# A hybrid S5 / gMLP encoder on one core: second tokens turned inside a product, last columns in two parts, S5 tiles pipelined, and 512 columns per matmul for the weights' first part

## The chip, the core and the metric

One NeuronCore of one Trainium2 chip runs the whole kernel. It has TensorE (matmul; the profile shows its weight loads apart as PEld), VectorE (DVE), ScalarE (ACT), GpSimd (POOL) and SyncE (SP), each with an instruction queue of its own, and 16 DMA engines. The metric is the device time in microseconds, the median of several runs. Beside it stands one profiled execution, from which all rows are read.

## The reference

A trunk of two layers over 256 tokens of 1024 channels, in float32. Each layer is three sub-layers, each followed by a layer normalisation of `alpha*x + sublayer(x)`: a SwiGLU feed-forward layer, a mixer (S5 state space model in layer 0, gMLP spatial gating in layer 1), and a second feed-forward layer.

```python
def _swiglu(x, w_in, w_out):
    gate, up = jnp.split(x @ w_in, 2, axis=-1)
    return (jax.nn.silu(gate) * up) @ w_out

for i in range(DEPTH):                       # DEPTH = 2, D_MODEL = 1024, D_FF = 2816
    h = _layernorm(DN_ALPHA * h + 0.5 * _swiglu(h, ffn_w_in[i, 0], ffn_w_out[i, 0]), ...)
    mix = _s5_mixer(h, ...) if i % 2 == 0 else _gmlp_mixer(h, ...)
    h = _layernorm(DN_ALPHA * h + mix, ...)
    h = _layernorm(DN_ALPHA * h + 0.5 * _swiglu(h, ffn_w_in[i, 1], ffn_w_out[i, 1]), ...)

# the end of the S5 mixer
y = jax.nn.gelu(y)
z = y * jax.nn.sigmoid(y @ w_glu + b_glu)
return z @ w_out
```

So the six sub-layers are FFN, S5, FFN, FFN, gMLP, FFN; the four feed-forward layers are called the first to the fourth below.

## The kernel before

Every product is done in three float32r products: an operand x is split into `hi`, its rounding to float32r, and `lo = x - hi`, and x*w is `xh*wh + xh*wl + xl*wh`. So each weight block of 128 x 2048 numbers that a DMA brings (`raw`) is rounded on ACT (`hi`) and subtracted on DVE (`lo`). `Stream` (`ws`) does that in order: `tick` finishes the subtraction that is pending, starts loads, and splits the next block while at most five split blocks are held; `done` gives a block free.

The tokens stand as `h[0]` and `h[1]`, 128 tokens each on the partitions. For a product over channels they are turned: `make_xt(t)` transposes `h[t]` on TensorE into a PSUM tile `tps`, ACT copies it (`xth`, line 192) and DVE subtracts (`xtl`, line 193). `xt` holds both token halves t and both parts j as `[128, t, j, 8 blocks k, 128]`.

A feed-forward layer goes over 11 chunks c of 256 hidden columns. In the three later layers the chunks 0 and 1 are done by `step_in(c, t)` for each token half with tokens as the stationary operand (lines 201 to 203, 512 columns); the second half of the tokens is turned after `step_in(1, 0)`. From chunk 2 on, and in the first layer from chunk 1 on, `chunk_in` has the weights as the stationary operand: for each of 2 m and 2 g (gate and up) and 8 k there are three products of 256 columns (both token halves), lines 208 to 210, one after another in one PSUM half-bank each. `act_t` then does silu on ACT (line 397) and the product with the up half on DVE (line 398); `split_gt` splits the result into `gt` (lines 406 and 407). `step_out` accumulates `gt` against the out weights into `acc` two chunks later, and `close` does the last three chunks' out products, the residual sum, the normalisation and, in between, the turning of the first tokens for the next sub-layer.

The normalisation of a token half (`layernorm_half`, `layernorm`, `rstd_of`, `normalize`): residual sum (line 239) and statistics (240) for each 512 columns, aggregate (247), on POOL the offset by epsilon (221) and the power -0.5 (222), meanwhile on DVE the subtraction of the mean (228), then the scaling (231). After the last one, two DMAs store each token half.

At the end of the S5 layer, `finish(n)` makes eight tiles of 128 channels ready for the out product: product with the gate (1164), rounding (1168 on DVE for three tiles, 1170 on ACT for five), remainder (1171). Two `rest(1)` between them do halves of a waiting weight split (119).

The order on every engine is that in which the program is written (a manual schedule); SBUF and PSUM tiles come from rotating pools (`mm_p`: four PSUM banks).

## Time and profile before

| | |
|---|---|
| median of 3 runs | 971.5 us (970.46 to 971.52) |
| profiled execution | 971.83 us, its span 969.7 us |
| busy, share of the span | TensorE 97%, weight loads 88%, DVE 67%, ACT 44%, POOL 17% |
| three 256-column products, lines 208 to 210 | 1184 each, 283 ns each |
| three 512-column out products of the FFNs, lines 201 to 203 | 352 each, about 390 ns each |
| read from HBM | 184.07 MB, 200 GB/s over the span with what is written |

The span is the time from the first to the last instruction. Durations of matmuls overlap, since they are pipelined: the distance between two starts says what one costs. Idle time of an engine costs something only where it ends on the path that the result waits for.

### The profile page before, as it was taken

How to read it: one execution, taken by the hardware profiler on the slowest of the kernel's cores; microseconds unless marked ns; L12 is line 12 of the kernel's file. 1: busy time of each engine (PE TensorE's matmuls, PEld its weight loads, DVE VectorE, ACT ScalarE, POOL GpSimd, SP SyncE). 2: the span in 40 equal slices, each digit the busy share in tenths (PEclk: the TensorE clock that was granted, in tenths of full speed). 3: DMA queues.
4: the chain of work that ended last, by engine and by line, in shares of the span. 5: the costliest groups of instructions: out<-in, count | busy, mean ns of one | idle time of the engine just before them, and what ended most of it. 6: DMA issues, size and time to landing. Idle time of an engine off the chain costs nothing.

```text
span 969.7 us, 16611 instructions
## 1 busy us (share of the span) xinstructions
PE 944.7 (97%) x6988; PEld 857.9 (88%) x6988; DVE 650.9 (67%) x805; ACT 426.5 (44%) x504; POOL 162.8 (17%) x240
## 2 busy tenths in 40 slices
PE   7999999999999999999999999999999999999996
PEld 5999999978896799999987999999889879999995
DVE  5889998787998774554667636455788866453635
ACT  5465347535342553434433534353445444444430
POOL 1888910011750100000001000000011010000001
PEclk9999999999999999999999999999999999999999
DMA  8887796958646566365547765636357468465521
GB/s 276 219 249 228 237 318 203 315 200 300 208 141 220 174 198 236 132 224 167 185 163 239 255 222 166 225 133 227 121 173 261 130 203 268 138 220 172 184 78 43
DMA packets 133898, 195.10 MB, mean 201 GB/s; under 512 B 7632, under 2 KB 104576, under 8 KB 133824
## 3 DMA queue, kind: packets, MB, share of 16 engines
q1 hardware_dynamic: 129152, 182.61, 56.8%
q0 software_dynamic: 4384, 10.92, 3.9%
q8 instruction: 54, 0.88, 0.4%
q10 hardware_dynamic: 288, 0.52, 0.1%
q14 instruction: 20, 0.16, 0.0%
HBM read 184.07 MB, written 9.96 MB: 200 GB/s over the span
## 4 chain that ended last, share of the span: by engine, by line
PE 68%; DVE 8%; ACT 2%; issue 1%; POOL 1%; DMA 1%; POOLq 0%; DVEq 0%; ACTq 0%
PE ips L210 11%; PE ips L209 11%; PE ips L208 11%; PE acc L201 7%; PE acc L202 7%; PE acc L203 7%; DVE lo L97 3%; PE pps L1080 2%; PE ips L203 1%; ACT hi L96 1%; DVE lo L89 1%; DMA raw<-in_s_w_in 1%; PE ips L201 1%; PE ips L202 1%; PE zps L209 1%
## 5 line engine op out<-in xcount | busy, mean ns | idle before, releaser
L210 PE MATMUL ips<-xt,lo 128*128 128x256 f32 x1184 | 335.2, 283 | 2.2 <-DVE lo L89 2.2
L208 PE MATMUL ips<-xt,hi 128*128 128x256 f32 x1184 | 335.4, 283 | 0.0
L209 PE MATMUL ips<-xt,hi 128*128 128x256 f32 x1184 | 335.0, 283 | 0.0
L89 DVE TENSOR_TENSOR lo<-raw,hi 128x2048 fp32r<-128x2048 f32 x107 | 242.9, 2291 | 8.7 <-ACT hi L88 8.3
L210 PEld LDWEIGHTS ips<-xt,lo 128*128 128x128 f32 x1184 | 227.1, 192 | 2.6 <-DVE lo L89 2.6
L208 PEld LDWEIGHTS ips<-xt,hi 128*128 128x128 f32 x1184 | 227.1, 192 | 1.5
L209 PEld LDWEIGHTS ips<-xt,hi 128*128 128x128 f32 x1184 | 227.1, 192 | 1.4
L88 ACT CAST hi<-raw 128x2048 fp32r<-128x2048 f32 x107 | 203.9, 1909 | 46.4 <-PE acc L203 26.6
L398 DVE TENSOR_TENSOR sgg<-ips,sgg 128x256 f32<-128x256 f32 x74 | 31.1, 420 | 166.1 <-ACT sgg L397 166.0
L201 PE MATMUL acc<-hi,gt 128*128 128x512 f32 x352 | 137.9, 392 | 0.2 <-ACT gt L406 0.2
L202 PE MATMUL acc<-lo,gt 128*128 128x512 f32 x352 | 137.4, 390 | 0.0
L203 PE MATMUL acc<-hi,gt 128*128 128x512 f32 x352 | 137.0, 389 | 0.0
L397 ACT ACTIVATE sgg<-ips 128x256 f32<-128x256 f32 x74 | 28.4, 383 | 216.4 <-PE ips L210 213.5
L221 POOL TENSOR_SCALAR rstd<-mv 128x1 f32<-128x1 f32 x14 | 10.4, 741 | 634.6 <-DVE mv L247 610.8
L97 DVE TENSOR_TENSOR lo<-raw,hi 128x2048 fp32r<-128x2048 f32 (+2 forms) x52 | 89.6, 1754 | 22.7 <-ACT hi L96 22.6
L203 PEld LDWEIGHTS acc<-hi,gt 128*128 128x128 f32 x352 | 66.1, 188 | 14.3 <-DVE gt L407 0.2
L201 PEld LDWEIGHTS acc<-hi,gt 128*128 128x128 f32 x352 | 66.2, 188 | 13.2 <-ACT gt L406 0.6
L202 PEld LDWEIGHTS acc<-lo,gt 128*128 128x128 f32 x352 | 66.3, 188 | 12.2
L96 ACT CAST hi<-raw 128x2048 fp32r<-128x2048 f32 (+2 forms) x52 | 74.5, 1482 | 4.2 <-DMA raw<-in_ffn_w_in 2.5
L407 DVE TENSOR_TENSOR gt<-sgg,gt 128x256 fp32r<-128x256 f32 x74 | 32.4, 438 | 61.8 <-ACT gt L406 61.8
L406 ACT CAST gt<-sgg 128x256 fp32r<-128x256 f32 x74 | 30.1, 406 | 58.2 <-DVE sgg L398 58.2
L201 PE MATMUL ips<-hi,xt 128*128 128x512 f32 x112 | 46.0, 410 | 3.6 <-ACT xt L192 2.3
(229 smaller groups left out, 1222.1 us busy)
## 6 DMA issues: line engine op xcount, KB each, us to landing
raw<-in_ffn_w_in SPq DMA_DIRECT2D x172, 512.0 KB, 5.7
raw<-in_ffn_w_out SPq DMA_DIRECT2D x44, 1024.0 KB, 5.1
raw<-in_g_w_in SPq DMA_DIRECT2D x8, 1024.0 KB, 6.0
rows<-w SPq DMA_DIRECT2D x8, 512.0 KB, 6.3
raw<-in_s_w_in SPq DMA_DIRECT2D x4, 1024.0 KB, 8.4
raw<-in_s_w_glu SPq DMA_DIRECT2D x4, 1024.0 KB, 5.0
w<-rows SPq DMA_DIRECT2D x8, 512.0 KB, 5.8
tc<-tc SPq DMA_DIRECT2D x16, 256.0 KB, 5.5
```

Source lines behind the costliest of these rows:

```text
L88: nc.scalar.copy(hi, raw)
L89: self.unfinished.append(lambda: nc.vector.tensor_tensor(lo, raw, hi.bitcast(F32), op=ALU.subtract))
L96: nc.scalar.copy(hi[:, s], raw[:, s])
L97: eng[p % len(eng)].tensor_tensor(lo[:, s], raw[:, s], hi[:, s].bitcast(F32), op=ALU.subtract)
L201: nc.tensor.matmul(ps, xh, wh, start=start, stop=False)
L202: nc.tensor.matmul(ps, xh, wl, start=False, stop=False)
L203: nc.tensor.matmul(ps, xl, wh, start=False, stop=stop)
L208: nc.tensor.matmul(ps, wh, xh, start=start, stop=False)
L209: nc.tensor.matmul(ps, wh, xl, start=False, stop=False)
L210: nc.tensor.matmul(ps, wl, xh, start=False, stop=stop)
L398: nc.vector.tensor_tensor(g, ps[:, 1], sg, op=ALU.mult)
L407: nc.vector.tensor_tensor(x[:, 1], g, x[:, 0].bitcast(F32), op=ALU.subtract)
```

## The change

Five edits.

1. In the later feed-forward layers chunks 2 to 10 go through `chunk_in2`: the weights' first part `wh` is multiplied with both parts of both token halves in one product of 512 columns (parts j side by side in a whole PSUM bank), and `wl` with the first part in one of 256 columns that adds to the first half of the bank. The two halves are added afterwards: an ACT copy of the second half to SBUF, and a DVE sum with the first, for gate and up each. The silu and the product with the up half then work from SBUF.
2. `make_xt(1)` at the start of these layers and of the gMLP is written into `step_in(1, 0)` / `step_v(1, 0)`, after the fifth of its eight k, ahead of the weight split that a `tick` issues there; the ticks of step (0, 0) split nothing.
3. `finish(n)` returns the remainder's instruction, which is issued after the next tile's product and rounding; for tiles 3 and 5 it is on POOL. `z` has four places instead of two. The two halves of a weight split come after tiles 4 and 5 instead of 1 and 3.
4. `rstd_of` adds epsilon on DVE instead of POOL.
5. The last normalisation has `close_last`: the last 512 columns of the last token half are accumulated for the last three chunks in two parts of 256 columns, in banks of their own, and the sum of the residual with what `acc` already holds is done before. The last step and its store are in three parts.

```diff
+    def mm2t(ps, wh, wl, k):
+        both = ps.rearrange("p j (t c) -> p j t c", t=2)
+        nc.tensor.matmul(both, wh, xt[:, :, :, k].rearrange("p t j c -> p j t c"), start=k == 0, stop=False)
+        nc.tensor.matmul(ps[:, 0], wl, xt[:, :, 0, k], start=False, stop=k == KD - 1)
...
-        nc.gpsimd.tensor_scalar(rstd[:, 0:1], mv[:, 1:2], eps, 1.0, op0=ALU.add, op1=ALU.mult)
+        nc.vector.tensor_scalar(rstd[:, 0:1], mv[:, 1:2], eps, 1.0, op0=ALU.add, op1=ALU.mult)
...
+    def close_last(acc, blocks, mm, gb, hscale, eps):
+        for t in range(2):
+            r = ln_p.tile([P, D], F32, tag="r", name="r", bufs=2)
+            parts = [(0, 512), (512, 512)] if t == 0 else [(0, 512), (512, 256), (768, 256)]
...
+            if t == 1:
+                s = slice(512, D)
+                nc.vector.scalar_tensor_tensor(r[:, s], in0=h[t][:, s], scalar=hscale, in1=acc[t][1], op0=ALU.mult, op1=ALU.add)
...
-        def step_in(c, t):
+        def step_in(c, t, mid=None, split=1):
             ps = mm_p.tile([P, 512], F32, tag="mm", name="ips")
-            in_mm(ids["in"][c], t, ps, range(4))
+            cut = 5 if mid else 4
+            in_mm(ids["in"][c], t, ps, range(cut))
+            if mid:
+                mid()
             if t:
                 finish_g()
-            ws.tick()
-            in_mm(ids["in"][c], t, ps, range(4, KD))
+            ws.tick(split)
+            in_mm(ids["in"][c], t, ps, range(cut, KD))
...
+        def chunk_in2(c):
+            for m in range(2):
+                sgg = g_p.tile([P, 2, SEQ], F32, tag="sgg", name="sgg")
+                for g in range(2):
+                    ps = mm_p.tile([P, 2, SEQ], F32, tag="mm", name="ips")
+                    for k in range(KD):
+                        wh, wl = ws.get(ids["in"][c][k // 4])
+                        s = slice(512 * (k % 4) + FC * g + P * m, 512 * (k % 4) + FC * g + P * m + P)
+                        mm2t(ps, wh[:, s], wl[:, s], k)
...
+                    split_gt()
+                    nc.scalar.copy(sgg[:, g], ps[:, 1])
+                    nc.vector.tensor_tensor(sgg[:, g], sgg[:, g], ps[:, 0], op=ALU.add)
+                    if g == 0:
+                        nc.scalar.activation(sgg[:, 0], sgg[:, 0], AF.Silu)
+                    else:
+                        nc.vector.tensor_tensor(sgg[:, 1], sgg[:, 1], sgg[:, 0], op=ALU.mult)
+                        later.append((new_gt(c, m), sgg[:, 1]))
...
-            step_in(0, 0)
-            step_in(1, 0)
-            make_xt(1)
+            step_in(0, 0, split=0)
+            step_in(1, 0, lambda: make_xt(1))
...
-            chunk_in(c)
+            (chunk_in if first else chunk_in2)(c)
...
-            z = buf["o"][n % 2][:, 0].rearrange("p q k -> p (q k)")
+            z = buf["o"][n % 2][:, n // 2 % 2].rearrange("p q k -> p (q k)")
...
-            V.tensor_tensor(yx(n, 1), z, yx(n, 0).bitcast(F32), op=SUB)
+            return lambda: (G if n in (3, 5) else V).tensor_tensor(yx(n, 1), z, yx(n, 0).bitcast(F32), op=SUB)
...
+        second = lambda: None
         for n in range(CT):
-            finish(n)
-            if n in (1, 3):
+            x = finish(n)
+            second()
+            second = x
+            if n in (4, 5):
                 rest(1)
+        second()
```

How the order moves, at three places. TensorE, where chunk 2 of the second feed-forward layer begins, behind the last products of chunk 1 (`ips` is the PSUM tile, `hi` and `lo` the parts of a weight block). Before:

```order
L201 MATMUL ips_3867<-hi48_3722,xt_96 128x512
L202 MATMUL ips_3867<-lo48_3723,xt_96 128x512
L203 MATMUL ips_3867<-hi48_3722,xt_96 128x512
L208 MATMUL ips_3915<-xt_96,hi49_3750 128x256
L209 MATMUL ips_3915<-xt_96,hi49_3750 128x256
L210 MATMUL ips_3915<-xt_96,lo49_3751 128x256
```

And now:

```order
L201 MATMUL ips_3867<-hi48_3722,xt_96 128x512
L202 MATMUL ips_3867<-lo48_3723,xt_96 128x512
L203 MATMUL ips_3867<-hi48_3722,xt_96 128x512
L216 MATMUL ips_3916<-xt_96,hi49_3795 128x512
L217 MATMUL ips_3916<-xt_96,lo49_3796 128x256
```

Three products per k became two, of which the first has 512 columns.

DVE at the start of the second feed-forward layer, from the last step of the S5 layer's normalisation (`h1`) on. Before:

```order
L231 SCALAR_TENSOR_TENSOR h1_95<-r_3668,rstd_3715,bet_3554 128x512 x2
L97 TENSOR_TENSOR lo48_3723<-raw48_3589,hi48_3722 128x512 x4
L97 TENSOR_TENSOR lo49_3751<-raw49_3602,hi49_3750 128x2048
L358 TENSOR_TENSOR sgg_3769<-ips_3737,sgg_3769 128x256
L358 TENSOR_TENSOR sgg_3797<-ips_3772,sgg_3797 128x256
L193 TENSOR_TENSOR xt_96<-tps_3800,xt_96 128x512
L193 TENSOR_TENSOR xt_96<-tps_3807,xt_96 128x512
```

And now:

```order
L238 SCALAR_TENSOR_TENSOR h1_95<-r_3668,rstd_3715,bet_3554 128x512 x2
L97 TENSOR_TENSOR lo48_3723<-raw48_3589,hi48_3722 128x512 x4
L399 TENSOR_TENSOR sgg_3762<-ips_3737,sgg_3762 128x256
L193 TENSOR_TENSOR xt_96<-tps_3781,xt_96 128x512
L193 TENSOR_TENSOR xt_96<-tps_3788,xt_96 128x512
L97 TENSOR_TENSOR lo49_3796<-raw49_3602,hi49_3795 128x2048
L399 TENSOR_TENSOR sgg_3811<-ips_3765,sgg_3811 128x256
```

The two subtractions for the turned tokens (`xt`) moved ahead of the whole weight split `lo49` and of the second step's gate product (`sgg`).

DVE in the middle of the S5 tiles (`rot` is z, `y` the activated output). Before, from tile 3's product:

```order
L1164 SCALAR_TENSOR_TENSOR rot<-rot,y 128x4x64
L1171 TENSOR_TENSOR xt<-rot,xt 128x2x128
L119 TENSOR_TENSOR lo_3490<-raw_3321,hi_3489 128x1024
L1164 SCALAR_TENSOR_TENSOR rot<-rot,y 128x4x64
L1171 TENSOR_TENSOR xt<-rot,xt 128x2x128
```

And now, from tile 3's product:

```order
L1236 SCALAR_TENSOR_TENSOR rot<-rot,y 128x4x64
L1243 TENSOR_TENSOR xt<-rot,xt 128x2x128
L1236 SCALAR_TENSOR_TENSOR rot<-rot,y 128x4x64
L119 TENSOR_TENSOR lo_3490<-raw_3321,hi_3489 128x1024
L1236 SCALAR_TENSOR_TENSOR rot<-rot,y 128x4x64
L1243 TENSOR_TENSOR xt<-rot,xt 128x2x128
```

The remainder that follows tile 3's product is now tile 2's; tile 3's own is on POOL, and the next one in the row is tile 4's.

More of the change, by code (lines that the diff above doesn't have):

```diff
@@ L274, in new_acc @@
         return [acc_p.tile([P, 512], F32, tag="acc", name="acc") for _ in range(2)]
+    def close_last(acc, blocks, mm, gb, hscale, eps):
+        for t in range(2):
+            r = ln_p.tile([P, D], F32, tag="r", name="r", bufs=2)
+            parts = [(0, 512), (512, 512)] if t == 0 else [(0, 512), (512, 256), (768, 256)]
+            step = parts[-1][1]
+            st = st_p.tile([P, D // step, 6], F32, tag="bst", name="bst")
+            if t == 1:
+                s = slice(512, D)
+                nc.vector.scalar_tensor_tensor(r[:, s], in0=h[t][:, s], scalar=hscale, in1=acc[t][1], op0=ALU.mult, op1=ALU.add)
+            for i, (c, w) in enumerate(parts):
+                s, n = slice(c, c + w), c // 512
+                ps = acc[t][n] if w == 512 else mm_p.tile([P, 512], F32, tag="mm", name="ops")[:, 0:w]
+                for j in range(len(blocks)):
+                    for kt in range(2):
+                        mm(j, t, n, kt, ps, (c % 512, w), w < 512 and j == 0 and kt == 0)
+                    if t == 0 and i == 0 and j < 2:
+                        ws.tick()
+                    if (t, i) == (1, len(parts) - 1):
+                        ws.done(blocks[j])
+                x, scale = (h[t], hscale) if w == 512 else (r, 1.0)
+                nc.vector.scalar_tensor_tensor(r[:, s], in0=x[:, s], scalar=scale, in1=ps, op0=ALU.mult, op1=ALU.add)
+                for x in range(c, c + w, step):
+                    nc.vector.bn_stats(st[:, x // step], r[:, x:x + step])
+            mv = st_p.tile([P, 2], F32, tag="mv", name="mv")
+            nc.vector.bn_aggr(mv, st)
+            rstd, (g, b) = rstd_of(mv, eps), gb
+            for n in range(2):
+                s = slice(512 * n, 512 * n + 512)
+                nc.vector.scalar_tensor_tensor(r[:, s], in0=r[:, s], scalar=mv[:, 0:1], in1=g[:, s], op0=ALU.subtract, op1=ALU.mult)
+            for i, (c, w) in enumerate(parts):
+                s = slice(c, c + w)
+                nc.vector.scalar_tensor_tensor(h[t][:, s], in0=r[:, s], scalar=rstd, in1=b[:, s], op0=ALU.mult, op1=ALU.add)
+                (nc.sync, nc.scalar)[i % 2].dma_start(out=out[0, P * t:P * t + P, s], in_=h[t][:, s])
@@ L276, in close @@
     def close(li, si, acc, blocks, mm, gb, hscale, eps, last):
+        if last:
+            return close_last(acc, blocks, mm, gb, hscale, eps)
         order = [(n, j) for n in range(2) for j in range(len(blocks))]
@@ L282, in close @@
                     mm(j, t, n, kt, acc[t][n])
-                    if (t, n, j, kt) == (1, 1, len(blocks) - 2, 0) and not last:
+                    if (t, n, j, kt) == (1, 1, len(blocks) - 2, 0):
                         make_xt(0, next_kind[li, si] == "s5")
@@ L290, in close @@
                     sums = layernorm_half(t, acc[t][0], 0, hscale)
-            if t == 1 and not last:
+            if t == 1:
                 ws.tick(1)
             layernorm(t, acc[t], gb, hscale, eps, sums)
-            if t == 1 and not last and next_kind[li, si] != "s5":
+            if t == 1 and next_kind[li, si] != "s5":
                 ws.tick(1, 4)
-            if last:
-                for n in range(2):
-                    s = slice(512 * n, 512 * n + 512)
-                    (nc.sync, nc.scalar)[n].dma_start(out=out[0, P * t:P * t + P, s], in_=h[t][:, s])
     def plan_ffn(li, fi, fine):
@@ L370, in step_in @@
                 done(ids["in"][c])
-            ws.tick()
+            ws.tick(split)
         def chunk_in(c):
@@ L439, in start_in, with mm_out @@
             done(ids["in"][0])
-        def mm_out(c, t, n, kt, ps):
+        def mm_out(c, t, n, kt, ps, cols=(0, 512), start=False):
             gh, gl = (gts[c, kt][:, j, P * t:P * t + P] for j in range(2))
             wh, wl = ws.get(ids["out"][c])
-            s = slice(D * kt + 512 * n, D * kt + 512 * n + 512)
-            mm3(ps, gh, gl, wh[:, s], wl[:, s], c == 0 and kt == 0, c == NCH - 1 and kt == 1)
+            s = slice(D * kt + 512 * n + cols[0], D * kt + 512 * n + sum(cols))
+            end = NCH - 4 if last and (t, n) == (1, 1) and cols[1] == 512 else NCH - 1
+            mm3(ps, gh, gl, wh[:, s], wl[:, s], start or c == 0 and kt == 0, c == end and kt == 1)
         def step_out(c, t):
@@ L479, in ffn @@
         c0 = NCH - 3
-        close(li, si, acc, [ids["out"][c] for c in range(c0, NCH)], lambda j, t, n, kt, ps: mm_out(c0 + j, t, n, kt, ps),
+        close(li, si, acc, [ids["out"][c] for c in range(c0, NCH)], lambda j, *args: mm_out(c0 + j, *args),
               gb, 2 * ALPHA, 4 * EPS, last)
```

23 lines of the change are left out of this document (16 added, 7 removed).

## The prediction

> **What bounds the kernel now.** I read the page's busy shares and its groups first, then the busy time in a stretch of a later feed-forward layer, then the spacing of single products in the timeline, and last the waits and the chain of waits at the places that the change touches. From the page:
>
> ```profile
> PE 944.7 (97%) x6988; PEld 857.9 (88%) x6988; DVE 650.9 (67%) x805; ACT 426.5 (44%) x504; POOL 162.8 (17%) x240
> ...
> L210 PE MATMUL ips<-xt,lo 128*128 128x256 f32 x1184 | 335.2, 283 | 2.2 <-DVE lo L89 2.2
> ```
>
> From the table of busy time by stretch, inside the second feed-forward layer (PE, weight load, DVE, ACT, POOL, granted clock, DMA share, GB/s):
>
> ```profile
> 333.00:500.00 167.00, 167.00 (x1148) 155.90 (x1147) 86.27 (x78) 70.88 (x76) 0.00 (x0) 1.00 0.56 187
> ```
>
> TensorE is never idle there, at full granted clock, while DVE is busy 52%, ACT 42% and the DMA engines 56%. One of the three 256-column products of the weights' first part has waited 2.2 us in the whole run. So TensorE sets the time, and its price is the distance between product starts, not the 283 ns that one lasts. First and last of a run of 256-column products, and of 512-column ones:
>
> ```profile
> 399.50 0.28 PE L208 MATMUL ips<-xt,hi 128*128 128x256 f32 x1
> ...
> 405.86 0.28 PE L210 MATMUL ips<-xt,lo 128*128 128x256 f32 x1
> ...
> 407.37 0.39 PE L201 MATMUL acc<-hi,gt 128*128 128x512 f32 x1
> ...
> 409.41 0.39 PE L201 MATMUL acc<-hi,gt 128*128 128x512 f32 x1
> ```
>
> 53 steps in 6.36 us are 0.120 us each; 9 steps in 2.04 us are 0.2267 us. Twice the columns cost 1.89 times, so per product some 13 ns do not depend on the columns (2 x 120 - 226.7 = 13.3).
>
> **The sum, part by part** (against the profiled execution: 971.83 us, span 969.7; the median is 971.5).
>
> *512 columns for the weights' first part.* Per k, three narrow products (3 x 0.120 = 0.360) become a wide and a narrow one (0.2267 + 0.120 = 0.347): 0.0133 us less. It happens 8 times for each of 4 column blocks in 9 chunks of three layers: 864 times, **11.5 us**, all on TensorE's path. Bounds: the rows price a wide product whose moving operand lies in one run, and a narrow one in two runs of 128; the new one has four runs. If the 13.3 ns were no fixed cost at all but the price of run breaks, a break would be 6.6 ns (120 = 256c + b and 226.7 = 512c give c = 0.443 ns, b = 6.6 ns) and the new product 246 ns: 864 x 0.006 = 5.5 us lost. At the other end, the narrow product costs nothing fixed after a wide one (107 ns): 23 us gained. I take the middle: each product brings a weight load of its own (6988 of each), which is reason enough for a fixed cost.
> The Trainium skill's page PSUM — Partial Sum Buffer, in Specifications (TRN2), says that any non-contiguous access pattern slows matmuls significantly; the accumulator's pattern stays contiguous here, and whether it holds for a moving operand in four runs no row here shows. By it this term would be a loss, by the rows' linear reading 11.5 us.
>
> *What the second half costs elsewhere.* Each block now has an ACT copy and a DVE sum more, 4 of each per chunk, and its own PSUM bank. Nearest rows:
>
> ```profile
> L398 DVE TENSOR_TENSOR sgg<-ips,sgg 128x256 f32<-128x256 f32 x74 | 31.1, 420 | 166.1 <-ACT sgg L397 166.0
> ...
> L406 ACT CAST gt<-sgg 128x256 fp32r<-128x256 f32 x74 | 30.1, 406 | 58.2 <-DVE sgg L398 58.2
> ```
>
> That is 1.7 us more DVE and 1.6 us more ACT in a chunk of 16.6 us: DVE 52 to 62%, ACT 42 to 52%. Cost zero, covered by four banks: a block takes 8 x 0.347 = 2.8 us, so a bank is wanted again 11.1 us after its first product and may be held 8.3 us after its last. The worst queue in front of a DVE sum is three weight splits in a row:
>
> ```profile
> 930.92 6.79 DVE L89 TENSOR_TENSOR lo<-raw,hi 128x2048 fp32r<-128x2048 f32 x3
> ```
>
> 6.8 + 0.4 + 0.4 = 7.6 us: 0.7 us under the limit, and in the new order a sum stands between those splits.
>
> *Second tokens turned inside a product.* At four places (three feed-forward layers, the gMLP) TensorE turns the second 128 tokens and then waits until ACT and DVE have copied them. The waits list, then the start of the second feed-forward layer in the timeline (start, duration, engine, line, and in brackets the idle time before and what ended it):
>
> ```profile
> PE tps L187 <- DVE h L231: 2.3, 2, 1.5
> ...
> PE ips L201 <- ACT xt L192: 2.3, 3, 0.8
> ...
> PE zps L201 <- DVE xt L193: 1.0, 1, 1.0
> ```
>
> ```profile
> 514.50 1.41 DVE L231 SCALAR_TENSOR_TENSOR h<-r,rstd,bet 128x512 f32<-128x512 f32 x2 [0.45 <-POOL rstd L222]
> 515.83 4.69 DVE L97 TENSOR_TENSOR lo<-raw,hi 128x512 fp32r<-128x512 f32 x5
> 520.44 0.75 DVE L358 TENSOR_TENSOR sgg<-ips,sgg 128x256 f32<-128x256 f32 x2
> 521.11 1.28 DVE L193 TENSOR_TENSOR xt<-tps,xt 128x512 fp32r<-128x512 f32 x2
> ...
> 519.22 1.03 PE L187 MATMUL tps<-ident,h 128*128 128x128 f32 x8
> ...
> 519.86 1.07 ACT L192 CAST xt<-tps 128x512 fp32r<-128x512 f32 x2
> ...
> 521.01 0.47 PE L201 MATMUL ips<-hi,xt 128*128 128x512 f32 x1 [0.75 <-ACT xt L192]
> 521.31 0.40 PE L202 MATMUL ips<-lo,xt 128*128 128x512 f32 x1
> 521.84 0.50 PE L203 MATMUL ips<-hi,xt 128*128 128x512 f32 x1
> ```
>
> 0.77 us for ACT, and 0.3 for DVE's part (521.84 instead of 521.31 + 0.23): 1.1 each, three times, and 1.0 at the gMLP. Moved nine products earlier (2.04 us), the turning starts at 517.2; the tokens are ready at 515.9, so nothing new is waited for. DVE has done its four weight pieces by 518.0 (4.69 less one split of 2.29) and both copies by 519.7, before the products that need them (520.1). Late next: the whole split that stood ahead of the copies now follows them, and on ACT its first half (1.90) ahead of the second activation. That activation's product reaches DVE only at about 523.2 (ACT 518.7 to 520.6, DVE split 2.29, product 0.4), while TensorE wants to turn it at 520.1 + 12 x 0.227 + 0.2 = 523.0. So a new wait of 0.3 (0 to 0.6). Net 3 x 0.8 + 1.0 = **3.4 us**.
>
> *S5 tiles pipelined.* Now each tile's product, copy and remainder follow one another and TensorE waits for the last three:
>
> ```profile
> 299.05 0.60 DVE L1164 SCALAR_TENSOR_TENSOR rot<-rot,y 128x256 f32<-128x256 f32 x1
> 300.18 0.43 DVE L1171 TENSOR_TENSOR xt<-rot,xt 128x256 fp32r<-128x256 f32 x1 [0.53 <-ACT xt L1170]
> ...
> 300.20 0.51 PE L201 MATMUL acc<-hi,xt 128*128 128x512 f32 x1 [0.50 <-ACT xt L1170]
> ...
> 303.16 0.50 PE L201 MATMUL acc<-hi,xt 128*128 128x512 f32 x1 [0.52 <-ACT xt L1170]
> ...
> 304.95 4.49 DVE L97 TENSOR_TENSOR lo<-raw,hi 128x2048 fp32r<-128x2048 f32 x2 [1.39 <-ACT hi L96]
> ```
>
> A tile takes 1.48 us (303.16 less 300.20, halved) where its three products need 0.68. With the remainder of the tile before put behind the next tile's product, DVE never waits for ACT; the sequence laid out with these durations ends near 300.6 instead of 303.6. Against it: tile 0's and 1's remainders come later, 0.75 us lost at the start. And two remainders go to POOL, which slows DVE. A POOL remainder, with the DVE split beside it and one alone:
>
> ```profile
> 287.60 0.76 POOL L1132 TENSOR_TENSOR xt<-y,xt 128x256 fp32r<-128x256 f32 x1 [2.45 <-ACT xt L1125]
> ...
> 287.69 1.76 DVE L119 TENSOR_TENSOR lo<-raw,hi 128x1024 fp32r<-128x1024 f32 x1
> ...
> 292.62 1.22 DVE L119 TENSOR_TENSOR lo<-raw,hi 128x1024 fp32r<-128x1024 f32 x1
> ```
>
> DVE loses 0.54 each time, which leaves it some 0.6 us ahead of TensorE. I get the first half of the out product 2.0 us earlier, and behind it the normalisation (after the 4.49 us of splits) by more than TensorE, so that its wait before turning the first tokens, 0.8 of the 2.3 us in the waits list, goes too: **2.8 us** (1.8 to 3.2).
>
> *Last columns in two parts, and the variance's offset on DVE.* The end now:
>
> ```profile
> 960.91 0.39 PE L203 MATMUL acc<-hi,gt 128*128 128x512 f32 x1
> 961.33 0.69 DVE L239 SCALAR_TENSOR_TENSOR r<-h,acc 128x512 f32<-128x512 f32 x1 [1.85 <-PE acc L203]
> 962.05 0.69 DVE L240 BATCH_NORM_STATS2 bst<-r 128x6 f32<-128x512 f32 x1
> 962.78 0.21 DVE L247 BATCH_NORM_AGGREGATE mv<-bst 128x2 f32<-128x12 f32 x1
> 963.03 1.42 DVE L228 SCALAR_TENSOR_TENSOR r<-r,mv,gam 128x512 f32<-128x512 f32 x2
> 963.08 0.75 POOL L221 TENSOR_SCALAR rstd<-mv 128x1 f32<-128x1 f32 x1 [6.38 <-DVE mv L247]
> 963.91 0.94 POOL L222 TENSOR_TENSOR rstd<-rstd,mhalf 128x1 f32<-128x1 f32 x1
> 964.89 1.41 DVE L231 SCALAR_TENSOR_TENSOR h<-r,rstd,bet 128x512 f32<-128x512 f32 x2 [0.44 <-POOL rstd L222]
> ```
>
> 18 wide products (4.08) become 36 narrow ones (4.32): +0.24. Sum and statistics over 256 instead of 512 columns: 0.42 and an estimated 0.4 instead of 0.72 and 0.73: -0.6. The offset on DVE (0.2, as the aggregate) instead of POOL's 0.75: the last step then follows the two L228 directly, -0.23. Three output steps instead of two +0.1, a last store of half the size an estimated -0.2: **0.7 us** (0 to 1.3). At the eleven other normalisations the offset is worth something only where TensorE waits for one: once more, before the S5 layer (1.5 us in the list): **0.2 us**. This may also be -0.2: POOL's 0.75 us for 128 numbers ended as the first L228 did, so POOL stood behind it, and the power will now arrive inside that instruction. By the Trainium skill's page SBUF — State Buffer, Who interferes with whom, the pair of ports is held for a whole instruction, and a second L228 that took it first would make the step 0.2 us later than now; the S5 rows above agree with such a hold (1.76 against 1.22).
>
> Sum: 11.5 + 3.4 + 2.8 + 0.7 + 0.2 = 18.6; 971.8 - 18.6 = 953.2, or 953 against the median.
>
> **The rivals.**
> - *The four runs eat the gain.* If a wide product takes as long as two narrow ones (0.240), the first term is zero: 971.5 - 7.1 = 964. At 0.246 it is -5.5: 970. For it: no row has such an operand. Against it: a two-run operand lies where one fixed cost per product puts it.
> - *Evacuation becomes the bound (slower).* ACT's copy, DVE's sum, ACT's activation follow each other across queues. If PSUM is held, TensorE waits in each of 27 chunks; the gain of 18.6 us is gone at 0.7 us per chunk, and at 1 us the time is 980. Against it: the banks' margin above, and 38% idle DVE.
> - *The new waits take what the old gave:* feed-forward starts and S5 give nothing: 959. For it: the split behind the copies; against it, all of it would have to come at each place.
> - *More than forecast:* narrow products behind wide ones at 107 ns: 864 x 0.013 more, 942.
>
> **How the numbers follow.** Forecast near 953 (946 to 962, the ends from a wide product of 0.237 and from half the extra gain): 0.78, the third rival within it. Four runs: 0.09, with 962 to 969.5 most of it. Evacuation: 0.05. Below 946: 0.05. No measurable change, within 0.2% (2 us, about what this measurement can tell): 0.03. So faster 0.92, same 0.03, slower 0.05, and 946 to 962 leaves out about 2 in 10.
>
> **What would show it.** Starts in a later layer should alternate 0.227 and 0.120; a wide one over 0.240 breaks the first term. TensorE should stay at 100% in the same stretches; waits of ips products on DVE or ACT would show the second rival. At the starts of these layers the waits on xt should be gone and a short one on the gate's transposes (L348 now) be there. In S5 the waits on L1170 should be gone. The end, from last product to last output step, should shrink by 0.8 us. Wrong I would be through the operand's runs above all.

## The result and the profile after

| | before | after |
|---|---|---|
| median of the runs | 971.5 us | 957.5 us (956.6 to 959.1) |
| ratio to before | | 0.9846 [0.9823, 0.987] |
| profiled execution, its span | 971.8, 969.7 us | 957.0, 955.2 us |

The change makes the kernel 14.0 us faster; 18.6 were forecast, and 953 (946 to 962). From the page after, the engines and the two products that took the place of three:

```profile
PE 937.7 (98%) x6142; PEld 813.9 (85%) x6142; DVE 693.5 (73%) x930; ACT 466.9 (49%) x612; POOL 155.7 (16%) x228
...
L216 PE MATMUL ips<-xt,hi 128*128 128x512 f32 x864 | 306.2, 398 | 0.0
...
L217 PE MATMUL ips<-xt,lo 128*128 128x256 f32 x864 | 242.5, 281 | 0.0
```

Neither product has waited for anything (0.0), and DVE went from 67 to 73%. The stretch of the second feed-forward layer that answers to the one before (same columns):

```profile
325.00:492.00 167.00, 166.81 (x865) 141.54 (x864) 102.28 (x116) 87.02 (x115) 0.00 (x0) 1.00 0.58 192
```

TensorE stays busy, at full clock, with DVE at 61% and ACT at 52%, where the prediction had 62 and 52. So the new copies and sums are hidden, and the question is the distance of starts. One block of eight k in the timeline, first and last pair, and the first product behind it:

```profile
397.71 0.40 PE L216 MATMUL ips<-xt,hi 128*128 128x512 f32 x1
397.95 0.28 PE L217 MATMUL ips<-xt,lo 128*128 128x256 f32 x1
...
400.18 0.40 PE L216 MATMUL ips<-xt,hi 128*128 128x512 f32 x1
400.41 0.28 PE L217 MATMUL ips<-xt,lo 128*128 128x256 f32 x1
400.53 0.40 PE L201 MATMUL acc<-hi,gt 128*128 128x512 f32 x1
400.77 0.40 PE L202 MATMUL acc<-lo,gt 128*128 128x512 f32 x1
```

Eight pairs take 2.82 us, 352.5 ns each, where 347 were forecast. Over all pairs the mean is 236.1 ns from a wide start to the narrow one and 116.8 ns from the narrow to the next wide: 352.9. The wide product costs 9 ns more than its 227, and the narrow one gives 3 back.

The start of the third feed-forward layer, where the second tokens are now turned inside a product, and the waits list:

```profile
510.63 1.03 PE L187 MATMUL tps<-ident,h 128*128 128x128 f32 x8
511.27 1.08 ACT L192 CAST xt<-tps 128x512 fp32r<-128x512 f32 x2 [3.40 <-PE tps L187]
511.42 0.48 PE L201 MATMUL ips<-hi,xt 128*128 128x512 f32 x1
511.88 1.29 DVE L193 TENSOR_TENSOR xt<-tps,xt 128x512 fp32r<-128x512 f32 x2
...
514.18 2.29 DVE L97 TENSOR_TENSOR lo<-raw,hi 128x2048 fp32r<-128x2048 f32 x1 [1.01 <-ACT hi L96]
...
516.86 0.44 PE L389 MATMUL tps<-ident,sgg 128*128 128x128 f32 x2 [0.19 <-DVE sgg L399]
```

```profile
PE tps L389 <- DVE sgg L399: 0.6, 3, 0.2
```

TensorE goes on with products of the first tokens (511.42, no wait) while ACT and DVE copy the second ones. The waits on L192 and L193 (2.3 and 1.0 us) are not in the list any more; the short wait on the gate's transposes is, 0.2 us once in each of three layers, where it was forecast: DVE does the 2.29 us split ahead of the gate's product. Whether that split is the reason is tested by e5_two_late.

The out product of S5, with the two remainders on POOL:

```profile
293.20 0.50 PE L203 MATMUL acc<-hi,xt 128*128 128x512 f32 x1 [0.23 <-DVE xt L1243]
...
294.25 1.86 POOL L1243 TENSOR_TENSOR xt<-rot,xt 128x256 fp32r<-128x256 f32 x1 [6.09 <-issue]
...
294.91 0.39 PE L201 MATMUL acc<-hi,xt 128*128 128x512 f32 x1
295.59 0.39 PE L201 MATMUL acc<-hi,xt 128*128 128x512 f32 x1
...
297.15 1.41 POOL L1243 TENSOR_TENSOR xt<-rot,xt 128x256 fp32r<-128x256 f32 x1 [1.05 <-ACT xt L1242]
```

Behind two waits of 0.2 us for DVE's remainder (the second in the first row) a tile of three products takes 0.68 us (295.59 less 294.91), the time of its products. And the end:

```profile
947.52 0.28 PE L203 MATMUL ops<-hi,gt 128*128 128x256 f32 x1
947.84 0.42 DVE L305 SCALAR_TENSOR_TENSOR r<-r,ops 128x256 f32<-128x256 f32 x1 [1.12 <-PE ops L203]
948.30 0.43 DVE L307 BATCH_NORM_STATS2 bst<-r 128x6 f32<-128x256 f32 x1
...
949.05 0.15 DVE L228 TENSOR_SCALAR rstd<-mv 128x1 f32<-128x1 f32 x1
949.12 1.41 DVE L313 SCALAR_TENSOR_TENSOR r<-r,mv,gam 128x512 f32<-128x512 f32 x2
949.35 0.92 POOL L229 TENSOR_TENSOR rstd<-rstd,mhalf 128x1 f32<-128x1 f32 x1 [6.97 <-DVE rstd L228]
950.45 1.53 DVE L316 SCALAR_TENSOR_TENSOR h<-r,rstd,bet 128x512 f32<-128x512 f32 x3
```

From the last product to the last normalising step it is 2.93 us, where it was 3.98 (964.89 less 960.91).

### The profile page after: what moved, and what is told of

Read it like the earlier page. It is cut to its first block, busy times and chain, and to the rows that moved or that the text cites. A ratio compares the mean times of both kernels' runs of the same rounds, so it can differ in the third digit from the quotient of the medians.

```text
span 955.2 us, 15164 instructions
## 1 busy us (share of the span) xinstructions
PE 937.7 (98%) x6142; PEld 813.9 (85%) x6142; DVE 693.5 (73%) x930; ACT 466.9 (49%) x612; POOL 155.7 (16%) x228
## 4 chain that ended last, share of the span: by engine, by line
PE 75%; DVE 2%; ACT 1%; POOL 0%; issue 0%; DVEq 0%; POOLq 0%; ACTq 0%
PE ips L216 21%; PE ips L217 11%; PE acc L203 8%; PE acc L201 8%; PE acc L202 8%; PE ips L203 2%; PE ips L201 2%; PE ips L202 2%; PE pps L1152 2%; PE tps L187 1%; PE zps L210 1%; PE zps L209 1%; PE zps L208 1%; PE ups L203 1%; PE ups L201 1%; PE ups L202 1%
## 5 line engine op out<-in xcount | busy, mean ns | idle before, releaser
L216 PE MATMUL ips<-xt,hi 128*128 128x512 f32 x864 | 306.2, 398 | 0.0
L216 PEld LDWEIGHTS ips<-xt,hi 128*128 128x128 f32 x864 | 162.3, 188 | 39.9
L217 PEld LDWEIGHTS ips<-xt,lo 128*128 128x128 f32 x864 | 163.1, 189 | 1.1
L201 PE MATMUL acc<-hi,gt 128*128 128x512 f32 x346 | 136.2, 394 | 0.5 <-ACT gt L476 0.5
L451 DVE TENSOR_TENSOR sgg<-sgg,ips 128x256 f32<-128x256 f32 x108 | 45.5, 421 | 124.5 <-ACT sgg L450 124.1
L203 PE MATMUL acc<-hi,gt 128*128 128x512 f32 x346 | 135.1, 391 | 0.0
L202 PE MATMUL acc<-lo,gt 128*128 128x512 f32 x346 | 134.9, 390 | 0.0
L229 POOL TENSOR_TENSOR rstd<-rstd,mhalf 128x1 f32<-128x1 f32 x14 | 13.3, 950 | 619.7 <-DVE rstd L228 619.7
L450 ACT COPY sgg<-ips 128x256 f32<-128x256 f32 x108 | 40.3, 373 | 115.7 <-PE ips L217 115.7
L208 PE MATMUL ips<-xt,hi 128*128 128x256 f32 x320 | 90.8, 284 | 0.0
L209 PE MATMUL ips<-xt,hi 128*128 128x256 f32 x320 | 90.5, 283 | 0.0
L201 PEld LDWEIGHTS acc<-hi,gt 128*128 128x128 f32 x346 | 65.0, 188 | 14.7 <-ACT gt L476 1.3
L203 PEld LDWEIGHTS acc<-hi,gt 128*128 128x128 f32 x346 | 64.9, 188 | 14.7 <-DVE gt L477 0.3
```

Of the source, the lines that this page charges most:

```text
L201: nc.tensor.matmul(ps, xh, wh, start=start, stop=False)
L202: nc.tensor.matmul(ps, xh, wl, start=False, stop=False)
L203: nc.tensor.matmul(ps, xl, wh, start=False, stop=stop)
L208: nc.tensor.matmul(ps, wh, xh, start=start, stop=False)
L209: nc.tensor.matmul(ps, wh, xl, start=False, stop=False)
L216: nc.tensor.matmul(both, wh, xt[:, :, :, k].rearrange("p t j c -> p j t c"), start=k == 0, stop=False)
```

## Where the 14.4 us of the span came from

Up to the S5 layer the same program varies by up to 4.6 us from one profiled execution to the next (213.37 to 217.96 in the table, where all the kernels but e11_offset_pool and the one before run the same code as the changed one), so I compare stages: from one start of the transposes of `h` (L187) in the timeline to the next, in us. "First" runs from the first transposes to the turning of the second tokens for S5, where "S5" starts; the other stages start with the turning of their first tokens. The fourth layer ends with its last product, "end" is what follows.

| kernel | first | S5 | FFN 2 | FFN 3 | gMLP | FFN 4 | end |
|---|---|---|---|---|---|---|---|
| before | 214.55 | 97.10 | 190.05 | 190.76 | 73.35 | 191.61 | 8.75 |
| after | 213.37 | 94.40 | 186.92 | 187.75 | 71.94 | 188.99 | 7.71 |
| e1_eight | 216.52 | 95.08 | 185.36 | 186.27 | 71.94 | 187.45 | 7.71 |
| e2_flat | 215.81 | 94.41 | 186.92 | 187.75 | 71.94 | 188.99 | 7.70 |
| e3_three | 215.42 | 95.10 | 188.34 | 189.21 | 71.95 | 190.48 | 7.78 |
| e4_two | 213.60 | 95.08 | 185.13 | 186.02 | 71.94 | 187.27 | 7.72 |
| e5_two_late | 213.92 | 95.08 | 184.73 | 185.64 | 71.95 | 186.82 | 7.70 |
| e6_four | 214.69 | 95.12 | 185.97 | 186.83 | 71.94 | 188.10 | 7.71 |
| e7_s5_undone | 216.16 | 97.62 | 184.93 | 185.64 | 71.95 | 186.82 | 7.71 |
| e8_xt_undone | 213.53 | 94.37 | 185.93 | 186.77 | 73.19 | 187.95 | 7.71 |
| e9_half | 213.79 | 94.43 | 186.83 | 187.84 | 71.94 | 189.06 | 7.71 |
| e10_close_undone | 215.19 | 94.36 | 184.73 | 185.63 | 71.93 | 186.48 | 8.28 |
| e11_offset_pool | 216.49 | 94.14 | 185.18 | 185.84 | 72.18 | 187.05 | 8.19 |
| e12_half_load | 217.96 | 94.41 | 183.30 | 184.23 | 71.94 | 185.47 | 7.71 |

Where a stage's code is the same, its length repeats within 0.2 us, but for S5, which comes out at 94.4 or 95.1. The traces show why. In the longer ones (e1, e3, e4, e5 and e6, and e7_s5_undone too) one GpSimd subtraction takes 2.56 us instead of 1.43, and TensorE waits 0.46 us for it. First e5_two_late, then the changed kernel:

```profile
283.16 2.35 DVE L119 TENSOR_TENSOR lo<-raw,hi 128x1024 fp32r<-128x1024 f32 x2
283.54 2.56 POOL L1208 TENSOR_TENSOR xt<-y,xt 128x256 fp32r<-128x256 f32 x1 [3.82 <-ACT xt L1201]
```

```profile
283.14 2.89 DVE L119 TENSOR_TENSOR lo<-raw,hi 128x1024 fp32r<-128x1024 f32 x2
283.52 1.43 POOL L1204 TENSOR_TENSOR xt<-y,xt 128x256 fp32r<-128x256 f32 x1 [3.82 <-ACT xt L1197]
```

Both start 0.38 us into the first of two DVE splits. In e5_two_late the subtraction ends 0.6 us behind the second split; in the changed kernel it ends 0.6 us behind the first (which ends at 284.36), and the two splits take 0.54 us more. So here the two engines did not work side by side: one stood still for the other, and which one went first differs between programs whose code is the same up to there.

The three later feed-forward layers gained 3.1, 3.0 and 2.6 us. Forecast were 3.8 (a third of 11.5) and 0.8 in each, so 1.5 to 1.6 are missing in each of the first two: the product term.

## The experiments

The ratios stand against runs of the kernel before on the same chip; their medians are 974.0 us for e1 to e4, 971.1 for e5 to e8, 971.7 for e9 to e11 and 971.1 for e12. Across these groups the stages say more than the medians.

**Is it the operand's runs, the alternation, or the evacuation?** Six kernels change these products alone: their order, their operand, their width or the place they write to.

e1_eight: the eight wide products of a block, then the eight narrow ones.

```diff
-                    for k in range(KD):
-                        wh, wl = ws.get(ids["in"][c][k // 4])
...
-                        mm2t(ps, wh[:, s], wl[:, s], k)
+                    for k0 in range(0, KD, 8):
+                        for part in range(2):
+                            for k in range(k0, k0 + 8):
+                                w = ws.get(ids["in"][c][k // 4])[part]
...
+                                mm2t(ps, w[:, s], k, part)
```

Part 0 is the wide product, part 1 the narrow one. In e4_two and e6_four below, the 8 is a 2 and a 4.

> The changed kernel with the eight wide products of a block first and its eight narrow ones after them (same products, same operands). In the changed kernel a wide product took 0.236 us to the next start and the narrow one behind it 0.117, 0.353 a pair, where 0.347 was forecast. Theory 'alternation': the 6 ns come from every change between widths. Then most pairs cost 0.227 + 0.120 = 0.347 here, 864 x 7/8 x 0.006 = 4.5 us less: span 950.7 instead of 955.2, about 953 us. Theory 'runs': the 6 ns come from the four runs of the wide operand. Then wide products stay at 0.236 or more behind each other and the time stays within 1 us of the changed kernel's 957.5.

Measured: 953.6 us (951.0 to 955.7), ratio 0.9794 [0.9766, 0.9821]. The timeline puts products of one line together:

```profile
397.52 2.00 PE L217 MATMUL ips<-xt,hi 128*128 128x512 f32 x8
399.36 1.12 PE L219 MATMUL ips<-xt,lo 128*128 128x256 f32 x8
400.32 2.00 PE L217 MATMUL ips<-xt,hi 128*128 128x512 f32 x8
```

A block takes 2.80 us and was 2.82; over all blocks a pair is 348.6 ns instead of 352.9, and each layer 1.5 us shorter (table). The wide products' mean distance is 229.5 ns and not 227: the first five after the narrow ones take 233, 236, 228, 233, 230 ns, and only then 227. The same operand in four runs then starts every 227 ns, so the runs cost nothing.

e2_flat: the wide product reads 512 numbers that lie in one run (other numbers than those needed).

```diff
-    nc.tensor.matmul(both, wh, xt[:, :, :, k].rearrange("p t j c -> p j t c"), ...)
+    nc.tensor.matmul(both.rearrange("p j t c -> p (j t c)"), wh, xt.rearrange("p t j k c -> p (t j k c)")[:, 512 * k:512 * k + 512], ...)
```

> The changed kernel, but a wide product reads 512 numbers of the turned tokens that lie in one run, other numbers than it should, so the result is not the reference's. Theory 'runs': wide and narrow together fall from 0.353 to 0.347, 864 x 0.006 = 5.2 us less, span 950.0, about 952 us. Theory 'alternation': no change, within 1 us of 957.5, wide starts still 0.236.

Measured: 957.9 us (956.7 to 958.9), ratio 0.9837 [0.9804, 0.987], 236.1 and 116.8 ns, and every stage from S5 on as after, to 0.01 us. With the row of e1_eight this ends the theory that four runs cost anything. The Trainium skill's page PSUM — Partial Sum Buffer, in Specifications (TRN2), says that a non-contiguous access pattern slows matmuls significantly. For a moving operand read from SBUF in four runs of 128 float32r numbers the trace does not agree: 236.1 ns, and 236.1 ns with one run. A broken pattern of the accumulator in PSUM, which the page is about, was not run.

e3_three: for seven of eight k the three narrow products of before, with the new evacuation kept.

```diff
-        nc.tensor.matmul(both, wh, xt[:, :, :, k].rearrange("p t j c -> p j t c"), start=k == 0, stop=False)
+        if k == 0:
+            nc.tensor.matmul(both, wh, xt[:, :, :, k].rearrange("p t j c -> p j t c"), start=True, stop=False)
+        else:
+            nc.tensor.matmul(both[:, 0], wh, xt[:, :, 0, k], start=False, stop=False)
+            nc.tensor.matmul(both[:, 1], wh, xt[:, :, 1, k], start=False, stop=False)
```

> The changed kernel with the three narrow products back for seven of eight k (the first k stays wide, since it opens the accumulation), the sum of the two halves kept. If the wide product is what gained 7.1 ns per k, this gives back 108 x 7 x 0.0071 = 5.4 us: span 960.6, about 963 us, with narrow starts 0.120 apart. If instead the copies and sums behind the blocks slow TensorE down (theory 'evacuation'), the narrow starts stand wider than 0.120 or waits show between blocks, and the time is over 965 us.

Measured: 962.9 us (959.7 to 963.6), ratio 0.9886 [0.9855, 0.9917]; narrow starts at 119.6 to 119.9 ns, as before, and no wait on ips. Each layer is 1.4 to 1.5 us longer than after. So the wide product is a gain, only a smaller one, and the evacuation costs nothing on the path.

e4_two: two wide, two narrow.

> The changed kernel with the products of two k taken together: two wide, two narrow, and so on, half as many changes between widths. Theory 'alternation': half the 6 ns are gone, 864 x 0.003 = 2.6 us less, span 952.6, about 955 us. Theory 'runs': within 1 us of 957.5.

Measured: 952.2 us (951.7 to 953.2), ratio 0.9784 [0.9757, 0.9812].

```profile
397.33 0.62 PE L217 MATMUL ips<-xt,hi 128*128 128x512 f32 x2
397.80 0.40 PE L219 MATMUL ips<-xt,lo 128*128 128x256 f32 x2
...
399.89 0.39 PE L219 MATMUL ips<-xt,lo 128*128 128x256 f32 x2
...
400.12 0.40 PE L201 MATMUL acc<-hi,gt 128*128 128x512 f32 x1
```

A block takes 2.79 us, a pair 348.3 ns (wide 233.1, narrow 115.3). Half as many changes of width save more than half of the excess: 4.6 of the 6.2 ns above the forecast's 346.7. So the cost is not one amount per change.

e6_four: four and four, and e9_half: as after, with the narrow product added to the bank's other half.

```diff
-    nc.tensor.matmul(ps[:, 0], wl, xt[:, :, 0, k], ...)
+    nc.tensor.matmul(ps[:, 1], wl, xt[:, :, 0, k], ...)     # e9_half
```

> Four wide then four narrow products, nothing else against e4_two. Theory one (a start that follows a change of width is late by a fixed amount, so the cost follows the count of changes, and the products after the block pay too): a pair costs about 348.5 ns, between 347.5 and 349, as at two and at eight; time 951.5 to 953.5 us. Theory two (only strict alternation costs, so that from two on all is alike): 348.4 ns and the same time as e4_two within 0.5 us. Theory three (fewer changes always gain): under 347.5 ns and 951 us or less.

> As the changed kernel (wide, narrow, wide, narrow), but the narrow product adds into the second half of the bank instead of the first; the two halves are summed afterwards as before, so the sum holds the same three products. Theory one (a product that follows one of another width starts off its steady distance, wherever it writes): wide to narrow 236 ns, narrow to wide 117 ns, 352.9 ns a pair, time 957.5 us within 1 us. Rival (the narrow product writes where the wide one has just written and waits for that, or the next wide one does): the distances change by 2 ns or more, in either direction, and the time moves by over 1.7 us.

Measured: e6_four 956.2 us (953.9 to 956.9), ratio 0.9839 [0.9819, 0.9859], 350.3 ns a pair (wide 231.9, narrow 118.4), layers 0.8 us longer than in e4_two. None of its three theories holds: one, two, four and eight in a row give 352.9, 348.3, 350.3 and 348.6 ns. e9_half 957.4 us (956.6 to 958.4), ratio 0.9861 [0.983, 0.9891], 236.2 and 116.8 ns: where the narrow product writes is no part of it.

**Is it the weight load?** Every product loads its own 128 columns of weights while the product ahead streams. The record of such a load lasts 188 ns in the changed kernel, and a narrow product starts only 117 ns before the next one. e12_half_load halves the load under the narrow product, for seven of eight k.

```diff
-    nc.tensor.matmul(both, wh, ...)
+    n = P if k == 0 else 64
+    nc.tensor.matmul(both[0:n], wh[:, 0:n], ...)
```

> As the changed kernel, but seven of the eight wide products of a block take only the first 64 columns of the weights' first part (so the load that lies under the narrow product ahead is half as long, and the sums of the other 64 output rows lack these products; the output is not the reference's). Theory one (the alternation costs because the full load of 128 weight columns has no slack under a 256-column product: 120 ns from start to start, 106.7 ns of that for the columns if the 13.3 are fixed): with half the load the pair goes to 347 ns or below, 6 us in all, about 951.5 us. Theory two (it follows from the change of width alone, whatever is loaded): pair 352 to 353.5 ns, 957.5 us within 1 us. The load's own rows should show whether it got shorter: 188 ns now.

Measured: 948.5 us (947.1 to 950.4), ratio 0.9757 [0.974, 0.9775]. The groups of weight loads in the second layer, by shape (busy time, mean ns), and the timeline:

```profile
L217 PEld LDWEIGHTS ips<-xt,hi 128*64 128x64 f32 x252 | 33.8, 134 | 10.0
...
L217 PEld LDWEIGHTS ips<-xt,hi 128*128 128x128 f32 x36 | 6.7, 187 | 1.4
```

```profile
398.90 0.39 PE L217 MATMUL ips<-xt,hi 128*64 128x512 f32 x1
...
399.12 0.28 PE L218 MATMUL ips<-xt,lo 128*128 128x256 f32 x1
399.13 0.13 PEld L217 LDWEIGHTS ips<-xt,hi 128*64 128x64 f32 x1
399.24 0.39 PE L217 MATMUL ips<-xt,hi 128*64 128x512 f32 x1
```

The load falls from 187 to 134 ns. Away from the full load at k = 0, a wide product then takes 227 and a narrow one 113 ns; with it the mean pair is 341.6 ns, and a layer is 3.5 to 3.6 us shorter than after. Right behind the one full load of a block stand 233, 117, 230, 114 ns: the old disturbance, once. The 341.6 ns lie below the 347 of theory one. So with the wide product's load halved the excess of the alternation goes, and with it half of the narrow product's fixed 13.3 ns (113.4 is 106.7 + 6.7, where 120 is 106.7 + 13.3). This points to the full load that lies under a narrow product, but does not prove it: the halved product also fills half of the output rows, and that was not told apart from the load. The Trainium skill's page TensorE: Matmul & The Clock Gate, in Back-to-back issue gap, says that the spacing in a stream of loads and products is set by both, pipelined. The trace agrees as far as it goes: products with the same moving columns came from 352.9 to 341.6 ns a pair with the halved load (and the halved output rows). Why two of each in a row hide a full load better than one or four is left open: no run shows it.

**The other parts.** e5_two_late takes e4_two and moves the split after the turning behind the activation; it is the base of the four that follow it. The expectation names the gMLP too, but the edit changes the feed-forward layers alone (gMLP 71.94 and 71.95).

```diff
-            ws.tick(split)
+            ws.tick(0 if mid else split)
```

> Two wide products then two narrow ones (as in e4_two), and in the second step of a later FFN and of gMLP the work of the split queue that stood between the turning of the second tokens and the next activation now stands behind that activation. Theory one (the gate transposes at a stage's start wait 0.34 to 0.35 us because VectorE and ScalarE do the split queue first): that wait at the three FFN starts is gone or under 0.1 us, each FFN is 0.3 us shorter than in e4_two, so about 951.2 us against 952.2. Theory two (the wait is the latency of the gate's own chain): wait still 0.3 us, 952.2 us, no difference from e4_two that can be measured.

Measured: 951.5 us (949.5 to 952.6), ratio 0.9793 [0.9776, 0.9809]; the three layers are 0.40, 0.38 and 0.45 us shorter than in e4_two. The gate's transposes come in one piece, without a wait:

```profile
514.81 0.60 PE L391 MATMUL tps<-ident,sgg 128*128 128x128 f32 x4
515.16 0.48 PE L201 MATMUL ips<-hi,xt 128*128 128x512 f32 x1
```

So the wait was the split that stood ahead. The medians of e4_two and e5_two_late are 0.8 us apart, which they can't tell; the stages can.

e8_xt_undone: the second tokens turned after the step again.

```diff
-            step_in(0, 0, split=0)
-            step_in(1, 0, lambda: make_xt(1))
+            step_in(0, 0)
+            step_in(1, 0)
+            make_xt(1)
...
-        pend = [step_v(0, 0, split=0), step_v(1, 0, lambda: make_xt(1))]
+        pend = [step_v(0, 0), step_v(1, 0)]
+        make_xt(1)
```

With it the weight splits of the first two steps come back to their old places, so this undoes the second edit as a whole.

> e5_two_late with the second tokens turned after the second step again, in the three later FFNs and in gMLP, and nothing else. By the forecast's term (3 times 1.1 us and 1.0 us, with the 0.3 us wait gone in both): 4.3 us slower, about 955.5 us, and TensorE waits on the turned tokens come back at four places, 0.9 to 1.2 us each. Rival (the turning itself, not its place, is what costs, so that the waits come back but are paid in the product's evacuation instead): under 2 us slower.

Measured: 956.2 us (954.7 to 956.5), ratio 0.984 [0.9826, 0.9855]: 4.7 us above e5_two_late. The stages give 1.20, 1.13, 1.24 and 1.13, also 4.7, and the waits are back (the first under another releaser's name):

```profile
PE ips L201 <- DVE sgg L401: 1.5, 3, 0.5
...
PE zps L201 <- DVE xt L193: 1.0, 1, 1.0
```

e7_s5_undone: each S5 tile finished at once again, remainders on DVE, and the halves of the weight split after tiles 1 and 3.

```diff
-            return lambda: (G if n in (3, 5) else V).tensor_tensor(yx(n, 1), z, yx(n, 0).bitcast(F32), op=SUB)
+            V.tensor_tensor(yx(n, 1), z, yx(n, 0).bitcast(F32), op=SUB)
...
-            x = finish(n)
-            second()
-            second = x
-            if n in (4, 5):
+            finish(n)
+            if n in (1, 3):
                 rest(1)
-        second()
```

> e5_two_late with the pipelining of the S5 tiles undone: each tile's finish is done at once, and the second part of each tile's split on VectorE again. By the forecast's term (2.8 us) and the landmarks of before and after (2.7 us): 2.7 us slower than e5_two_late, about 954 us, and the gap between the starts of the h transposes around S5 grows from 94.4 back to 97.1 us, with TensorE's waits on the finishing line back. Rival (the S5 gain came from elsewhere, for instance from the shorter start): less than 1 us slower.

Measured: 954.2 us (952.8 to 956.1), ratio 0.9824 [0.9807, 0.9842], 2.7 us above e5_two_late; S5 takes 97.62 instead of 95.08 (both with the 2.56 us subtraction). The wait of before is back:

```profile
PE acc L201 <- ACT xt L1246: 1.5, 3, 0.5
```

e10_close_undone: the last 512 columns in one part. e11_offset_pool: the offset on GpSimd.

```diff
-        if last:                                            # e10_close_undone
-            return close_last(acc, blocks, mm, gb, hscale, eps)
-        nc.vector.tensor_scalar(rstd[:, 0:1], mv[:, 1:2], eps, ...)   # e11_offset_pool
+        nc.gpsimd.tensor_scalar(rstd[:, 0:1], mv[:, 1:2], eps, ...)
```

> e5_two_late with the last columns of the last layer in one part of 512 again, by the same closing routine as the other layers, and nothing else. By the forecast's term (0.7 us) and the landmarks of before and after (0.24 us of products saved, 1.05 us from the last product to the end lost): 0.8 us slower at the end of the trace, 952.3 us against 951.5, which a measurement of this size can barely tell; in the trace the stretch from the last product to the end is 8.7 us instead of 7.7. Rival (the shorter end came from the offset on VectorE alone): the stretch stays near 7.9 us.

> e5_two_late with the variance's offset on GpSimd again, and nothing else. By the forecast: 0.2 us slower before the S5 layer and 0.2 us at the end, 951.9 us against 951.5, within what can be told. Rival (GpSimd's power, which now comes inside VectorE's step instead of behind it, waits for the ports): 0.2 us faster per normalisation that is waited for. The trace decides, by the distance from the variance to the last normalising step.

Measured: e10_close_undone 951.8 us (949.1 to 952.4), ratio 0.9794 [0.9766, 0.9822], no difference that the times can tell. In the stages the end is 0.58 us longer and the products before it 0.34 us shorter: a net 0.24. The end of 8.28 us lies between the 8.7 that was expected, which counted the offset's share as well, and the rival's 7.9: columns and offset both have a part in it. e11_offset_pool 954.9 us (952.5 to 957.0), ratio 0.983 [0.98, 0.9861]: slower by more than either theory expected, though its first two stages together were 1.6 us slower, which may be their usual variation. From the second layer on it loses 0.45, 0.20, 0.23, 0.23 and, at the end, 0.49 us. The normalisation behind the second layer, in e11_offset_pool and then in e5_two_late:

```profile
496.35 1.41 DVE L237 SCALAR_TENSOR_TENSOR r<-r,mv,gam 128x512 f32<-128x512 f32 x2
496.41 0.74 POOL L230 TENSOR_SCALAR rstd<-mv 128x1 f32<-128x1 f32 x1 [170.31 <-DVE mv L256]
497.24 0.95 POOL L231 TENSOR_TENSOR rstd<-rstd,mhalf 128x1 f32<-128x1 f32 x1
498.22 1.42 DVE L240 SCALAR_TENSOR_TENSOR h<-r,rstd,bet 128x512 f32<-128x512 f32 x2 [0.46 <-POOL rstd L231]
```

```profile
494.33 1.40 DVE L237 SCALAR_TENSOR_TENSOR r<-r,mv,gam 128x512 f32<-128x512 f32 x2
494.57 0.93 POOL L231 TENSOR_TENSOR rstd<-rstd,mhalf 128x1 f32<-128x1 f32 x1 [170.79 <-DVE rstd L230]
495.65 1.41 DVE L240 SCALAR_TENSOR_TENSOR h<-r,rstd,bet 128x512 f32<-128x512 f32 x2
```

From the start of L237 to that of L240 it is 1.87 us with the offset on GpSimd and 1.32 with it on DVE: the bracketed wait of 0.46 is gone. The rival, by which the power inside DVE's step costs time, does not hold.

## Why the prediction was right, and the term that was not

| term | forecast | measured | from |
|---|---|---|---|
| 512 columns | 11.5 | 6.1 | 864 x (360 - 352.9) ns |
| tokens turned inside a product | 3.4 | 3.5 | e8_xt_undone 4.7, less the new wait of 1.2 (e5_two_late) |
| S5 tiles | 2.8 | 2.5 to 2.7 | e7_s5_undone; stages of before and after, which hold the offset before S5's end too |
| last columns and end | 0.7 | 0.7 | 0.24 (e10_close_undone) and 0.49 for the offset there (e11_offset_pool) |
| offset elsewhere | 0.2 | 1.1 | e11_offset_pool, four stages after S5 |

The measured terms sum to 13.9 to 14.1 us, against 14.0 between the medians. The terms that rest on e5_two_late are priced in its order and not in that of the changed kernel; that they sum so well is no proof of each. Stage by stage they fit as well: 2.04 us of products in each layer, the turned tokens less the new wait, the offset and, in the last layer, the 0.34 us lost give 3.29, 2.99, 1.47 and 2.61 us for the second layer, the third, the gMLP and the fourth, and the changed kernel gained 3.13, 3.01, 1.41 and 2.62.

- **The step that failed** is the price of the new pair, "a wide and a narrow one (0.2267 + 0.120 = 0.347)": it measures 0.3529, and the term 6.1 us instead of 11.5. Both prices were read from runs of products of one width, where they hold. That a pair can't be priced from them showed already in the trace of before: behind narrow products its first 512-column ones start 233, 236, 228 ns apart and not 227. I took the row from the middle of such a run. The measured 236.1 lies just inside the end "0.237" of the likeliest case's own range, and so the time stayed in it, with help from the offset (below). The lower end was worked out wrongly: half the extra gain of 11.5 us leads to 947 and not to 946.
- **The reason for the fixed cost**, "each product brings a weight load of its own", is borne out by e12_half_load, where half the load goes with half the fixed cost. But the reading was half done: the prediction did not ask what a full load under a shorter product does to the products around it. That the load and not the output rows makes the excess is likely and not shown.
- **The four runs** of the operand, "above all" what was feared, cost nothing (e2_flat). The chance of 0.09 went to the wrong mechanism for a wide product that is too slow.
- **Evacuation** was costed right, at nothing, with the DVE and ACT shares forecast (61 and 52% against 62 and 52).
- **Second tokens and the new wait**: right in place and in size. The new wait cost 0.38 to 0.45 us a layer where 0.3 was said, and its cause, the split, is shown by e5_two_late. (The rows at 514 to 521 us, from which this term was worked out, are the start of the third feed-forward layer and not of the second; in the second the same waits stand.)
- **S5**: right in size. The POOL remainders took 1.86 and 1.41 us and not the 0.76 of the row that I used: each ended 0.6 us behind the DVE split beside it, and so did the one of 0.76, which began shortly before a split's end. DVE lost what was forecast: its product behind the first of them took 1.17 us instead of 0.61. TensorE did not wait for them.
- **The offset** was undervalued, and it hid a part of the miss. I counted it, at 0.2 us, only where a wait was seen in the trace of before. Inside the later layers and the gMLP it was worth 0.2 to 0.45 us a stage in the order of e5_two_late; that it shows there because TensorE no longer stands still for the copies is my reading. The feared delay, that DVE goes first once more and the power comes later, did not come: with the offset on DVE the last step starts 0.55 us earlier. The Trainium skill's page SBUF — State Buffer, Who interferes with whom, makes the pair of ports that VectorE and GpSimd share an exclusive lock, so the power would have to wait. The traces agree with a wait, but behind one DVE instruction alone. After the change the power begins inside the first of the two subtractions of the mean, and it takes 0.92 to 0.94 us where 0.51 to 0.52 of that one is left and 0.99 to 1.01 where 0.57 to 0.58 is left: it ends some 0.4 us behind it. With the offset on GpSimd (e11_offset_pool) the offset ends 0.05 us behind the first subtraction, and the power, which begins 0.53 before the end of the second, 0.4 behind that one. So by these rows GpSimd stood behind two DVE instructions before, and behind one now.

The best version that leaves nothing out is, by its stages, e5_two_late, the changed kernel with two wide and two narrow products in turn and, in each later feed-forward layer, one split moved: 951.5 us, ratio 0.9793 [0.9776, 0.9809] against 0.9846 [0.9823, 0.987]. The times alone can't tell it from e4_two (0.9784) or e10_close_undone (0.9794).

## What to carry to other kernels

The start distance of a matmul is a property of its neighbours too: read it from a place where the same two widths follow each other, even if that is only the few products at a seam. Where short and long products share a bank, try them in pairs before taking them in turn, since the order costs nothing else. And when a wait is taken away, price the small edits again with it gone: a chain that was hidden behind it comes to the surface.

## What the runs showed of the hardware that was not expected

- 512- and 256-column float32r products, each with a load of 128 columns: 346.7 ns a pair by the distances within runs of one width, but 352.9 in turn, 348.3 two by two, 350.3 four by four and 348.6 eight by eight. In turn the distances come round every three pairs: 233, 117, 241, 120, 236, 113 ns.
- With a load of 64 columns under the narrow product (and 64 output rows of the wide one) the narrow one's start distance goes from about 117 to 113.4 ns and the disturbance of the wide ones goes, but for the pairs right behind a full load; the record of the load falls by 53 ns.
- Four runs of 128 numbers in the moving operand cost the same as one of 512, to 0.1 ns in the mean.
- A GpSimd subtraction of 128x256 numbers that met a DVE weight split ended 0.6 us behind that split, so in S5 it took 0.76 us, 1.43 or, where a second split went first as well, 2.56; where it went ahead of the second split, DVE lost 0.54 us.
